# One more weight buffer for the experts: a gate rebuilt late, and SwiGLU's intermediate values left in PSUM

## The chip, the cores and the metric

The kernel runs on one core of a Trainium2 chip. The metric is device microseconds for one execution. Three runs of the kernel before took 1690.12, 1691.52 and 1692.07 us, median 1691.52.

## The reference, cut to what matters

Two transformer blocks over 256 tokens of width 1024, in fp32. The first has two attention branches and a mixture of 32 experts, four per token. The second is dense. The change touches the experts, and the gate `g_m` that multiplies their sum.

```
mod = silu(c) @ w_ada + b_ada
sh_a, sc_a, g_a, sh_m, sc_m, g_m = split(mod, 6)
x = x + g_a * merge(attention branches)
h = rmsnorm(x, norm_mlp) * (1 + sc_m) + sh_m
# for each of a token's 4 experts e
gate = min(h @ w_gate[e] + b_gate[e], 7)
up   = clip(h @ w_up[e] + b_up[e], -7, 7)
act  = (up + 1) * (gate * sigmoid(1.702 * gate))
y   += weight[e] * (act @ w_down[e] + b_down[e])
x = x + g_m * y                       # then the second block
```

## The kernel before, in words

**Stages.** The attention stage (to about 294 us of the profile) ends with the output projection and the router: `rwa` are the router's weights scaled by the gains, and L1233 holds its 16 matmuls, which read `rwa`. Then `moe()` runs the experts' stage (to about 1218 us), and `block2()` the second block.

**Experts.** They are done in 16 pairs. The two experts of a pair run side by side on the two column halves of TensorE (tiles `128*64`), 64 slots each. For pair p the program is written in this order: `gate(p)`, `scatter(p-2)`, `prep1`/`prep2(p+1)` (gather the next pair's tokens, matmuls L1341), `up(p)`, `prep3(p+1)` (two transposes L1358, two matmuls L1363), `down(p-1)`, `trans(p)` (transposes L1471). A scheduler reorders each engine's instructions by its own estimates; in most pairs it puts `prep3` between `gate(p)` and `up(p)`. Each of gate, up and down is 64 matmuls of 128x512 (L1431) into two PSUM banks, one for each half h of the 1024 columns.

**PSUM.** There are 8 banks. Four hold the running sum `acc` through the whole stage. The other four (`bank_a`) go round among gate, prep2, up, prep3, down and trans. A matmul that starts in a bank waits until the last reader of what stood there is done. The banks of `gate(p)` are next used by `prep3`: L1358 takes that of h=0, L1363 that of h=1. The banks of `up(p)` are next used by `down(p-1)`.

**SwiGLU.** After gate, for each h: a clip by VectorE (L1448, bank to SBUF tile `gs`), a sigmoid by ScalarE (L1449, `gs` to SBUF tile `e2`, shown as e), a product by VectorE (L1450). After up: a clip (L1459, bank to `e2`) and a fused (u+1)*g (L1460, `e2` and `gs` to `gs`). The last reader of a bank is thus the clip, L1448 or L1459.

**Weights.** Each gate, up or down of a pair is 8 loads of 1 MB, issued by SyncE's queue (SP) in one fixed list: gate(p), up(p), down(p-1). `fill()` issues the next load as soon as fewer than `room` tiles live. The first 12 expert loads go to the ring of 12 buffers, the next EXTRA (7) to the pool `more`, which `moe()` opens at L1262 in the space that the closed pools of the attention stage (`p1` among them) have left. I number the expert loads #1, #2, ...: #1 to #8 are gate(0), #9 to #16 up(0), #17 to #24 gate(1); #13 to #19 are the first in `more`. A load waits for the last user of its buffer's bytes, and all loads behind it on SP wait too. With 19 tiles, #20 waits until gate(0) frees a ring buffer.

**Overflow.** After pair 6 a branch (L1523) asks whether some expert has more than 64 tokens. At it SP waits until all its outstanding loads have landed before it issues the next.

**Gate g_m.** `gm_b` is g_m on all partitions. Its row is made in the attention stage: `add_row` adds `b_ada` (two small DMAs on ScalarE's queue, `brow`), `bcast_rows` splits it (mh, ml) and spreads it by four K=1 matmuls (L726, L727). It stays in the pool `keep` until L1659, after the last scatter. The same numbers stand as columns in `mod`.

**End of the stage.** `down(14)`, bias products L1409, scatter(14) L1514/L1515, `down_last` for pair 15 (L1498), in halves.

Of the kernel before, what the change touches and what calls it, by code (L numbers as in the profile page):

```python
# [25 lines left out]
AHEAD = 5  # L26
EXTRA = 7
OVER_AT = 6
# [47 lines left out]
def build(tc, I, out):  # L76
# [14 lines left out]
    def bank(which="a", dt=F32, shape=(128, 512)):  # L91
        return psp.tile(list(shape), dt, name="bank_" + which, tag="bank")
# [337 lines left out]
    mod = keep.tile([128, 3, 4, 4, 2], F32, name="mod")  # L430
    gm_b = keep.tile([128, D], F32, name="gm_b")
    kc = keep.tile([128, 256], F32, name="kc")
# [83 lines left out]
    def body():  # L516
# [142 lines left out]
        def ada_one():  # L659
# [36 lines left out]
            if g == 1:  # L696
                grow = cg.rearrange("p k t d -> p (k t d)")
                add_row(grow, 0, mrow, 0)
                late["row"] = grow
            if g == 2:  # L700
                add_row(mrow, 2, mrow, 1)
                late["rows"] = mrow

# [429 lines left out]
        while ada_queue:  # L1133
            ada_one()
        spreads = bcast_rows(ga_b, 0, late["row"]), bcast_rows(gm_b, 2, late["rows"])
        yb_hi, yb_lo = late["yb"][:, 0], late["yb"][:, 1]
# [121 lines left out]
    def moe(pl, parts, routed):  # L1258
# [44 lines left out]
        def token_weights():  # L1303
            V.tensor_reduce(out=sm[:, :, 0], in_=pr, axis=AX.X, op=OP.add)
            V.reciprocal(sm[:, :, 1], sm[:, :, 0])
            V.tensor_tensor(pr, pr, sm[:, :, 1:2].to_broadcast([128, 2, 4]), op=OP.mult)
            V.tensor_tensor(eq, eq, pr.unsqueeze(3).to_broadcast([128, 2, 4, 32]), op=OP.mult)
            V.tensor_reduce(out=wt, in_=eq.rearrange("p t k e -> p t e k"), axis=AX.X, op=OP.add)
            t = m1.tile([128, 2, 32], F32, name="w3t")
            V.tensor_copy(w3[:, :, 0], wt)  # L1310
            V.tensor_tensor(t, wt, w3[:, :, 0], op=OP.subtract)
            V.tensor_copy(w3[:, :, 1], t)
            V.tensor_tensor(t, t, w3[:, :, 1], op=OP.subtract)
            V.tensor_copy(w3[:, :, 2], t)
# [127 lines left out]
        def gate(p):  # L1442
            ps = expert_mm("gate", p, xg_of(p), "b_gate")
            g = scr([128, 1024], "gs", "wh")
            for h in range(2):
                g_ = g[:, 512 * h:512 * h + 512]
                s_ = m1.tile([128, 512], F32, name="e2", tag="e2")
                V.tensor_scalar(out=g_, in0=ps[h], scalar1=7.0, scalar2=None, op0=OP.min)  # L1448
                S.activation(s_, g_, AF.Sigmoid, scale=1.702)  # L1449
                V.tensor_tensor(g_, g_, s_, op=OP.mult)  # L1450
            state["g", p] = g

        def up(p):
            ps = expert_mm("up", p, xg_of(p), "b_up")
            g = state["g", p]
            for h in range(2):
                g_ = g[:, 512 * h:512 * h + 512]
                u_ = m1.tile([128, 512], F32, name="e2", tag="e2")
                V.tensor_scalar(out=u_, in0=ps[h], scalar1=7.0, scalar2=-7.0, op0=OP.min, op1=OP.max)  # L1459
                V.scalar_tensor_tensor(out=g_, in0=u_, scalar=1.0, in1=g_, op0=OP.add, op1=OP.mult)  # L1460

# [59 lines left out]
        def overflow():  # L1521
            nv = nc.values_load(nov[0:1, 0:1], min_val=0, max_val=16)
            with tc.If(nv > 0):  # L1523
                with tc.For_i(0, nv, 1):
                    oh = m1.tile([128, 96], F32, name="oh")
                    eb = m1.tile([128, 8], F32, name="eb")
                    V.scalar_tensor_tensor(out=oh, in0=oidx, scalar=it, in1=ov, op0=OP.is_equal, op1=OP.mult)
                    jk = m1.tile([128, 96], F32, name="jk")
                    V.scalar_tensor_tensor(out=jk, in0=oh, scalar=1.0, in1=eid, op0=OP.mult, op1=OP.mult,
# [6 lines left out]
                    ev = nc.sync.value_load(ei[0:1, 0:1], min_val=0, max_val=NE - 1)  # L1536
                    one = m1.tile([128, 32], F32, name="one")
                    V.tensor_scalar(out=one, in0=iota[:, :32], scalar1=eb[:, 0:1], scalar2=None, op0=OP.is_equal)
                    jk2 = m1.tile([128, 32], F32, name="jk2")
                    for tt in range(2):  # L1540
# [38 lines left out]
                    def block_bias(nm, h):  # L1579
                        t = scr([64, 512], "bb", "wl")  # L1580
                        nc.sync.dma_start(out=t, in_=sl[nm][bass.ds(ev, 1), 512 * h:512 * h + 512].to_broadcast([64, 512]))
                        return t

                    for h in range(2):
                        ps = block_mm("gate", lambda j: xo[:, j], h)
                        bt = block_bias("b_gate", h)
                        g_ = m1.tile([64, 512], F32, name="e2", tag="e2")
                        V.tensor_tensor(g_, ps, bt, op=OP.add)
                        V.tensor_scalar(out=g_, in0=g_, scalar1=7.0, scalar2=None, op0=OP.min)
                        s_ = scr([64, 512], "s_", "wl")  # L1590
                        S.activation(s_, g_, AF.Sigmoid, scale=1.702)
                        V.tensor_tensor(g_, g_, s_, op=OP.mult)
                        ps = block_mm("up", lambda j: xo[:, j], h)
                        bt = block_bias("b_up", h)
                        u_ = scr([64, 512], "u_", "wl")
                        V.tensor_tensor(u_, ps, bt, op=OP.add)
# [14 lines left out]
        for p in range(NPAIR):  # L1611
# [35 lines left out]
        for h in range(2):  # L1647
# [8 lines left out]
            for tt in range(2):  # L1656
                s = slice(512 * h, 512 * h + 512)
                t = m1.tile([128, 512], F32, name="e2", tag="e2")
                V.tensor_tensor(t, acc[tt][h], gm_b[:, s], op=OP.mult)  # L1659
                V.tensor_tensor(x_sb[:, tt, s], x_sb[:, tt, s], t, op=OP.add)  # L1660
# [418 lines left out]
```

## Time and profile before

| | |
|---|---|
| median of three runs | 1691.52 us |
| the profiled execution's own time | 1692.38 us |
| its span | 1690.7 us |
| PE busy | 1627.3 us (96%) |
| DVE, ACT busy | 694.0 us (41%), 465.5 us (28%) |
| HBM read | 534.75 MB, 317 GB/s over the span |
| 1 MB loads of w_up, w_down: median us from issue to landing | 19.5, 19.5 |

The page's 40 slices are 42.3 us each. The matmuls' ends are modelled, so PE's busy share doesn't say that PE is the bound; the starts are measured. A row of the timeline joins like instructions that follow each other: start, length, line, operation, tiles, count, and in brackets the idle time before the first with what ended it.

### The profile page before, as it was taken

What the parts mean: (1) busy time and instruction counts of PE and PEld (TensorE: products, weight loads), DVE (VectorE), ACT (ScalarE), POOL (GpSimd) and SP (SyncE); (2) the same over time, 40 slices, a digit from 0 to 9 for tenths busy, and PEclk for the clock granted to TensorE, in tenths of its full rate; (3) what the DMA queues carried; (4) which work ended last, traced back from release to release, by engine and by line L of the source; (5) the groups of instructions that cost most, each with busy time, mean ns of one, the idle gap of its engine ahead of it and who ended that gap; (6) DMA issues with size and microseconds to landing.
All of it is one profiled execution on the core that took longest, in us unless ns stands there. A gap on an engine that the chain in (4) does not pass through costs nothing. (4 is left out here: it accounts for less than half of the span.)

```text
span 1690.7 us, 22289 instructions
## 1 busy us (share of the span) xinstructions
PE 1627.3 (96%) x9091; PEld 1019.3 (60%) x9091; DVE 694.0 (41%) x1350; ACT 465.5 (28%) x769; POOL 88.9 (5%) x120
## 2 busy tenths in 40 slices
PE   8999999999999999899999999999999999999997
PEld 5877887444433443444344334434488899989996
DVE  4999986221111112111121121111367556665555
ACT  3445663010100100010001000000256445454443
POOL 3012200000000000000000000000004101100001
PEclk9999999999999999999999999999999999999999
DMA  9654668999999999999999999999963333565530
GB/s 377 252 189 150 208 249 358 391 424 425 425 426 424 426 425 425 383 425 424 426 425 425 425 425 426 425 423 425 403 244 112 133 132 124 184 218 181 176 146 25
DMA packets 117155, 537.29 MB, mean 318 GB/s; under 512 B 11882, under 2 KB 13622, under 8 KB 66874
## 3 DMA queue, kind: packets, MB, share of 16 engines
q1 hardware_dynamic: 112160, 532.19, 78.5%
q10 hardware_dynamic: 4458, 3.46, 0.7%
q8 instruction: 72, 1.18, 0.3%
q14 instruction: 33, 0.27, 0.0%
q0 software_dynamic: 432, 0.19, 0.0%
HBM read 534.75 MB, written 1.05 MB: 317 GB/s over the span
## 5 line engine op out<-in xcount | busy, mean ns | idle before, releaser
L1431 PE MATMUL bank_a<-w,xg 128*64 128x512 f32 x2048 | 520.4, 597 | 1.0 <-DMA w<-in_w_up_dram 1.0
L1431 PEld LDWEIGHTS bank_a<-w,xg 128*64 128x64 f32 x2048 | 183.5, 137 | 276.4 <-issue 254.6
L319 DVE TENSOR_TENSOR wl<-w,wh 128x1024 fp32r<-128x1024 f32 (+1 forms) x193 | 236.5, 1231 | 153.7 <-ACT wh L316 143.4
L316 ACT ACTIVATE wh<-w 128x1024 fp32r<-128x1024 f32 (+1 forms) x193 | 201.9, 1049 | 216.3 <-PE bank_a L389 88.1
L1431 PE MATMUL bank_a<-w,at 128*64 128x512 f32 x960 | 229.7, 595 | 8.0 <-DVE e L1459 5.3
L390 PE MATMUL bank_a<-hi,wl 128*128 128x256 f32 x640 | 180.3, 283 | 1.0 <-DVE wl L319 1.0
L388 PE MATMUL bank_a<-hi,wh 128*128 128x256 f32 x616 | 176.3, 287 | 1.1 <-ACT hi L474 0.6
L389 PE MATMUL bank_a<-lo,wh 128*128 128x256 f32 x616 | 174.3, 283 | 0.2 <-DVE lo L475 0.2
L1431 PEld LDWEIGHTS bank_a<-w,at 128*64 128x64 f32 x960 | 83.3, 137 | 149.6 <-issue 103.7
L513 ACT ACTIVATE y<-bank_a,ws 128x512 fp32r<-128x512 f32 x32 | 22.0, 688 | 444.8 <-PE bank_a L1431 430.1
L390 PEld LDWEIGHTS bank_a<-hi,wl 128*128 128x128 f32 x640 | 122.3, 192 | 1.4 <-DVE wl L319 1.4
L388 PEld LDWEIGHTS bank_a<-hi,wh 128*128 128x128 f32 x616 | 117.8, 192 | 3.2 <-issue 0.9
L389 PEld LDWEIGHTS bank_a<-lo,wh 128*128 128x128 f32 x616 | 118.1, 192 | 0.9 <-DVE lo L475 0.6
L514 DVE SCALAR_TENSOR_TENSOR y<-bank_a,ws,y 128x512 fp32r<-128x512 f32 x32 | 24.0, 751 | 221.9 <-ACT y L513 220.3
L1459 DVE TENSOR_SCALAR e<-bank_a 128x512 f32<-128x512 f32 x32 | 22.1, 691 | 185.7 <-PE bank_a L1431 184.1
L1449 ACT ACTIVATE e<-gs 128x512 f32<-128x512 f32 x32 | 20.2, 630 | 236.5 <-DVE gs L1448 224.9
L1341 PEld LDWEIGHTS bank_a<-gr,x_sb 128*128 128x128 f32 x512 | 64.2, 196 | 23.0 <-issue 19.5
L1448 DVE TENSOR_SCALAR gs<-bank_a 128x512 f32<-128x512 f32 x32 | 22.0, 691 | 134.5 <-PE bank_a L1431 114.2
L1341 PE MATMUL bank_a<-gr,x_sb 128*128 128x128 f32 x512 | 69.3, 286 | 0.7 <-DVE gr L1324 0.7
L1346 DVE TENSOR_SCALAR xg<-bank_a,abp 128x128 f32<-128x128 f32 x64 | 21.9, 404 | 106.9 <-PE bank_a L1341 106.9
L1349 ACT ACTIVATE xg<-bank_a,abp 128x128 f32<-128x128 f32 x64 | 24.3, 456 | 121.9 <-PE bank_a L1341 121.8
L354 PE MATMUL bank_b<-wh,hh 128*128 128x512 f32 x128 | 49.9, 390 | 0.0
(468 smaller groups left out, 2220.7 us busy)
## 6 DMA issues: line engine op xcount, KB each, us to landing
w<-in_w_up_dram SPq DMA_DIRECT2D x144, 1024.0 KB, 19.5
w<-in_w_down_dram SPq DMA_DIRECT2D x136, 1024.0 KB, 19.5
w<-in_w_gate_dram SPq DMA_DIRECT2D x128, 1024.0 KB, 17.9
w<-in_w_in_dram SPq DMA_DIRECT2D x44, 1024.0 KB, 8.0
w<-in_w_ada_dram SPq DMA_DIRECT2D x16, 1024.0 KB, 6.6
w<-in_w_ada_dram SPq DMA_DIRECT2D x16, 512.0 KB, 9.2
w<-in_w_out_dram SPq DMA_DIRECT2D x8, 1024.0 KB, 8.9
w<-in_w_down_dram SPq DMA_DIRECT2D x16, 512.0 KB, 10.9
```

Source lines behind the costliest of these rows:

```text
L316: split_last[0] = S.activation(r32(wh[:, :n]), t[:, o:o + n], AF.Copy)
L319: V.tensor_tensor(r32(wl[:, :n]), t[:, o:o + n], wh[:, :n], op=OP.subtract)
L354: PE.matmul(o, r32(sh), r32(mh), start=first, stop=False)
L388: PE.matmul(o, r32(wh[:, k, c]), r32(hi[:, j]), start=j == 0 and m % 2 == 0, stop=False)
L389: PE.matmul(o, r32(wh[:, k, c]), r32(lo[:, j]), start=False, stop=False)
L390: PE.matmul(o, r32(wl[:, k, c]), r32(hi[:, j]), start=False, stop=j == 7 and m % 2 == 1)
L513: S.activation(r32(hi), src, AF.Copy, scale=scale)
L514: V.scalar_tensor_tensor(out=r32(lo), in0=src, scalar=scale, in1=hi, op0=OP.mult, op1=OP.subtract)
L1341: PE.matmul(ps[:, k], x_sb[:, tt, o:o + 255:2], d["gr"][:, tt].rearrange("p e s -> p (e s)"), start=tt == 0, stop=tt == 1)
L1349: S.activation(xg[:, j], ps[:, k], AF.Identity, bias=abp_[:, 1, j:j + 1], scale=abp_[:, 0, j:j + 1])
L1431: state["mm"] = PE.matmul(ps[h][64 * ab:64 * ab + 64], lhs(j, ab), w[ab][:, e, 512 * h:512 * h + 512], start=bias is None and j == 0, stop ...
L1459: V.tensor_scalar(out=u_, in0=ps[h], scalar1=7.0, scalar2=-7.0, op0=OP.min, op1=OP.max)
```

## The change

EXTRA goes from 7 to 8, so that 20 tiles live. To free the space: `gm_b` moves from `keep` to `p1` (only as the accumulator of its column sums; in `p1` it stands between `ga_b` and `rwa`), and `gate_rows()` makes it anew at p=15 from `mod`: per half one VectorE copy that repeats the columns, four 128x128 matmuls with the identity, one ScalarE copy to `gm_b`. `add_row` for g_m and its `bcast_rows` go. The tile `e2` goes: the sigmoid is written to the bank that the clip has read, and the clip of up stays in its bank. `w3t` and the scratch of the overflow loop move into other tiles.

```diff
-EXTRA = 7
+EXTRA = 8
-    gm_b = keep.tile([128, D], F32, name="gm_b")
         ga_b = p1.tile([128, D], F32, name="ga_b")
+        gm_b = p1.tile([128, D], F32, name="gm_b")
         rwa = p1.tile([128, 8, 32], F32, name="rwa")
-            if g == 2:
-                add_row(mrow, 2, mrow, 1)
-                late["rows"] = mrow
-        spreads = bcast_rows(ga_b, 0, late["row"]), bcast_rows(gm_b, 2, late["rows"])
+        spreads = (bcast_rows(ga_b, 0, late["row"]),)
@@ gate(p)
-                s_ = m1.tile([128, 512], F32, name="e2", tag="e2")
                 V.tensor_scalar(out=g_, in0=ps[h], scalar1=7.0, scalar2=None, op0=OP.min)
-                S.activation(s_, g_, AF.Sigmoid, scale=1.702)
-                V.tensor_tensor(g_, g_, s_, op=OP.mult)
+                S.activation(ps[h], g_, AF.Sigmoid, scale=1.702)
+                V.tensor_tensor(g_, g_, ps[h], op=OP.mult)
@@ up(p)
-                V.tensor_scalar(out=u_, in0=ps[h], scalar1=7.0, scalar2=-7.0, op0=OP.min, op1=OP.max)
-                V.scalar_tensor_tensor(out=g_, in0=u_, scalar=1.0, in1=g_, op0=OP.add, op1=OP.mult)
+                V.tensor_scalar(out=ps[h], in0=ps[h], scalar1=7.0, scalar2=-7.0, op0=OP.min, op1=OP.max)
+                V.scalar_tensor_tensor(out=g_, in0=ps[h], scalar=1.0, in1=g_, op0=OP.add, op1=OP.mult)
+        def gate_rows():
+            gm_b = late["gm"] = m2.tile([128, D], F32, name="gm_b", tag="xg")
+            rest = late["rest"] = m2.tile([128, 2, 512], F32, name="rest", tag="xg")
+            for h in range(2):
+                rd = rest[:, h].rearrange("p (i n) -> p i n", i=4)
+                V.tensor_copy(rd, mod[:, 2, :, 2 + h, 0].unsqueeze(2).to_broadcast([128, 4, 128]))
+                ps = bank("a")
+                for i in range(4):
+                    PE.matmul(ps[:, 128 * i:128 * i + 128], rd[:, i], ident, start=True, stop=True)
+                S.copy(gm_b[:, 512 * h:512 * h + 512], ps)
...
                     bias_products()
+                    gate_rows()
```

Three places show how it moves instructions. The first is SP's queue at loads #13 to #20. In a row stand the line, the operation, the tile with its source, and the counters waited for (DVE, PE, Pool, Activation: engines; DMAHW, DMASW: earlier DMAs). Before:

```order
L206 DMA w_3173<-in_w_up_dram 128x2048 [waits DMASW3_49,DMASW4_49,DMASW2_49,DMAHW1_49,DMASW1_49,PE_49]
L206 DMA w_3175<-in_w_up_dram 128x2048 [waits DMAHW2_49,Pool_49]
L206 DMA w_3177<-in_w_up_dram 128x2048 [waits DMAHW3_49]
L206 DMA w_3179<-in_w_up_dram 128x2048 [waits DMAHW4_49]
L206 DMA w_3181<-in_w_gate_dram 128x2048 [waits DMAHW5_49,DVE_49,PE_49]
L206 DMA w_3183<-in_w_gate_dram 128x2048 [waits DVE_49,DMAHW6_49,PE_49,Activation_49]
L206 DMA w_3185<-in_w_gate_dram 128x2048 [waits DMAHW7_49]
L206 DMA w_3338<-in_w_gate_dram 128x2048 [waits DMAHW0_49,PE_49]
```

The same eight loads now:

```order
L206 DMA w_3156<-in_w_up_dram 128x2048 [waits DMAHW7_49,DVE_49,PE_49]
L206 DMA w_3158<-in_w_up_dram 128x2048 [waits DMAHW0_49,Pool_49]
L206 DMA w_3160<-in_w_up_dram 128x2048 [waits DMAHW1_49]
L206 DMA w_3162<-in_w_up_dram 128x2048 [waits DMAHW2_49]
L206 DMA w_3164<-in_w_gate_dram 128x2048 [waits DMAHW3_49,DVE_49]
L206 DMA w_3166<-in_w_gate_dram 128x2048 [waits DMAHW4_49,DVE_49,Activation_49]
L206 DMA w_3168<-in_w_gate_dram 128x2048 [waits DMAHW5_49]
L206 DMA w_3170<-in_w_gate_dram 128x2048 [waits DMASW4_49,DMASW3_49,DMAHW6_49,DMASW2_49,DMASW1_49]
```

The waits for the software DMAs have gone from #13 to #20, and #13 now waits for VectorE. In the built program the pool `more` begins lower: #13's buffer is bytes 163616 to 171808 of each partition, over `ga_b` (161024 to 165120), `gm_b` and `rwa` (169216 to 170240); before it was 171040 to 179232, over `rw` and the small tables behind `rwa`. #13's counts are those of L1242, which reads `ga_b`, and of the last router matmul (L1231, which was L1233). Before, #13's PE count was that of the small matmuls L1206, and the last router matmul stood at #18. #20 no longer waits for PE.

The second place is TensorE between gate and up of pair 2. Before:

```order
L1431 MATMUL bank_a_3754<-w_3651,xg_3586 64x512
L1358 LDWEIGHTS gb_3829
L1358 MATMUL bank_a_3918<-kh_80,gb_3829 128x128 [waits DVE_49]
L1358 LDWEIGHTS gb_3829
L1358 MATMUL bank_a_3918<-kh_80,gb_3829 128x128
L1363 LDWEIGHTS gb_3829
L1363 MATMUL bank_a_3923<-w3_3307,gb_3829 128x96 [waits DVE_49]
L1363 LDWEIGHTS gb_3829
L1363 MATMUL bank_a_3923<-w3_3307,gb_3829 128x96
L1431 MATMUL bank_a_3858<-w_3653,xg_3586 64x512 [waits DMAHW5_49]
```

The same place now (L1356 and L1361 were L1358 and L1363, L1429 was L1431):

```order
L1429 MATMUL bank_a_3730<-w_3619,xg_3564 64x512
L1429 MATMUL bank_a_3832<-w_3629,xg_3564 64x512 [waits DMAHW3_49]
L1429 MATMUL bank_a_3833<-w_3629,xg_3564 64x512
L1356 LDWEIGHTS gb_3803 [waits DVE_49]
L1356 MATMUL bank_a_3890<-kh_79,gb_3803 128x128 [waits PE_49]
L1356 LDWEIGHTS gb_3803
L1356 MATMUL bank_a_3890<-kh_79,gb_3803 128x128
L1361 LDWEIGHTS gb_3803 [waits DVE_49]
L1361 MATMUL bank_a_3895<-w3_3292,gb_3803 128x96 [waits PE_49]
L1361 LDWEIGHTS gb_3803
L1361 MATMUL bank_a_3895<-w3_3292,gb_3803 128x96
L1429 MATMUL bank_a_3832<-w_3631,xg_3564 64x512 [waits DMAHW4_49]
```

Two instructions of up, both for the same expert of the pair (tile w_3629), have moved ahead of prep3. Each wait for VectorE is for the last reader of gate's bank, the clip before and the product now.

The third place is TensorE at the end of the stage, before and now:

```order
L1431 MATMUL bank_a<-w,xg 64x512 x32
L1431 MATMUL bank_a<-w,at 64x512 x2
L1471 MATMUL bank_a<-ident,gs 128x128 x8
L1431 MATMUL bank_a<-w,at 64x512 x30
L1409 MATMUL bank_b<-bd,wtt 128x512 x4
L1514 MATMUL bank_b<-y,sc 128x512
L1515 MATMUL bank_b<-y,sc 128x512
```

```order
L1429 MATMUL bank_a<-w,xg 64x512 x30
L1429 MATMUL bank_a<-w,at 64x512 x32
L1407 MATMUL bank_b<-bd,wtt 128x512 x4
L1486 MATMUL bank_a<-ident,rest 128x128 x8
L1467 MATMUL bank_a<-ident,gs 128x128 x8
L1523 MATMUL bank_b<-y,sc 128x512
L1524 MATMUL bank_b<-y,sc 128x512
```

The eight transposes of pair 15 have moved from within down(14) to behind it, and the eight matmuls of `gate_rows` stand before them.

## Rows read from the trace of the kernel before

**Rows 1.** What the DMA engines moved, GB/s in 40 slices of the span.
```profile
GB/s 377 252 189 150 208 249 358 391 424 425 425 426 424 426 425 425 383 425 424 426 425 425 425 425 426 425 423 425 403 244 112 133 132 124 184 218 181 176 146 25
```

**Rows 2.** Timeline of PE, pair 2 and the start of pair 3 (columns as told above).
```profile
407.05 0.24 PE L1363 MATMUL bank_a<-w,gb 128*128 128x96 bf16 x2 [0.56 <-DVE gs L1448]
407.23 14.01 PE L1431 MATMUL bank_a<-w,xg 128*64 128x512 f32 x64
...
422.68 13.95 PE L1431 MATMUL bank_a<-w,at 128*64 128x512 f32 x62 [0.45 <-DVE e L1459]
...
465.29 0.24 PE L1363 MATMUL bank_a<-w,gb 128*128 128x96 bf16 x2 [0.56 <-DVE gs L1448]
```

**Rows 3.** Timeline of DVE beside rows 2.
```profile
405.45 0.69 DVE L1448 TENSOR_SCALAR gs<-bank_a 128x512 f32<-128x512 f32 x1 [4.31 <-PE bank_a L1431]
406.31 0.69 DVE L1448 TENSOR_SCALAR gs<-bank_a 128x512 f32<-128x512 f32 x1 [0.17 <-PE bank_a L1431]
406.92 0.68 DVE L1450 TENSOR_TENSOR gs<-gs,e 128x512 f32<-128x512 f32 x1
...
420.41 0.69 DVE L1459 TENSOR_SCALAR e<-bank_a 128x512 f32<-128x512 f32 x1 [11.42 <-PE bank_a L1431]
421.13 0.69 DVE L1460 SCALAR_TENSOR_TENSOR gs<-e,gs 128x512 f32<-128x512 f32 x1
421.93 0.69 DVE L1459 TENSOR_SCALAR e<-bank_a 128x512 f32<-128x512 f32 x1
```

**Rows 4.** Timeline of ACT beside rows 2.
```profile
406.23 0.63 ACT L1449 ACTIVATE e<-gs 128x512 f32<-128x512 f32 x1 [13.56 <-DVE gs L1448]
```

**Rows 5.** Waits of PE, 300 to 1190 us: total us, times, longest us.
```profile
PE bank_a L1363 <- DVE gs L1448: 6.2, 11, 0.6
PE bank_a L1431 <- DVE e L1459: 5.3, 11, 0.8
```

**Rows 6.** Timeline of PE, pairs 10 and 14.
```profile
866.39 0.25 PE L1363 MATMUL bank_a<-w,gb 128*128 128x96 bf16 x2 [0.56 <-DVE gs L1448]
...
1101.49 0.24 PE L1363 MATMUL bank_a<-w,gb 128*128 128x96 bf16 x2 [0.56 <-DVE gs L1448]
```

**Rows 7.** Timeline of SP's queue around the start of the experts' stage.
```profile
272.64 2.52 SPq L206 DMA_DIRECT2D w<-in_w_up_dram  x5
...
285.35 0.81 SPq L206 DMA_DIRECT2D w<-in_w_gate_dram  x2
297.77 0.80 SPq L206 DMA_DIRECT2D w<-in_w_gate_dram  x2
```

**Rows 8.** Waits of SP's queue, 284 to 286 us.
```profile
SPq L206 <- PE bank_b L1233: 1.6, 1, 1.6
```

**Rows 9.** Windows: us, engines' busy us, granted clock, DMA share, GB/s.
```profile
296.00:298.00 2.00, 2.00 (x12) 0.56 (x9) 0.00 (x0) 0.00 (x0) 0.00 (x0) 1.00 0.00 0
```

**Rows 10.** Timeline of PE and DVE behind the overflow branch.
```profile
689.26 4.04 PE L1341 MATMUL bank_a<-gr,x_sb 128*128 128x128 f32 x32
697.62 0.41 PE L1422 MATMUL bank_a<-b_up,sel 96*64 96x512 bf16 x2 [4.32 <-DVE gs L1448]
698.22 0.61 PE L1422 MATMUL bank_a<-b_up,sel 96*64 96x512 bf16 x2 [0.19 <-DVE gs L1448]
...
696.88 1.29 DVE L1448 TENSOR_SCALAR gs<-bank_a 128x512 f32<-128x512 f32 x2 [20.31 <-SPq L1523]
```

**Rows 11.** Timeline of PE at the end of the experts' stage.
```profile
1153.86 9.05 PE L1431 MATMUL bank_a<-w,xg 128*64 128x512 f32 x36
...
1172.68 0.73 PE L1471 MATMUL bank_a<-ident,gs 128*128 128x128 f32 x4
...
1174.85 7.63 PE L1431 MATMUL bank_a<-w,at 128*64 128x512 f32 x32
...
1193.04 3.69 PE L1409 MATMUL bank_b<-bd,wtt 32*128 32x512 f32 x8
```

**Rows 12.** Timeline of PE at the K=1 matmuls of `bcast_rows`.
```profile
231.54 0.41 PE L727 MATMUL bank_b<-ml,ones 1*128 1x512 f32 x4
```

More of the change, by code (lines that the diff above doesn't have):

```diff
@@ L1308, in token_weights @@
             V.tensor_reduce(out=wt, in_=eq.rearrange("p t k e -> p t e k"), axis=AX.X, op=OP.add)
-            t = m1.tile([128, 2, 32], F32, name="w3t")
+            t = lg
             V.tensor_copy(w3[:, :, 0], wt)
@@ L1457, in up @@
                 g_ = g[:, 512 * h:512 * h + 512]
-                u_ = m1.tile([128, 512], F32, name="e2", tag="e2")
-                V.tensor_scalar(out=u_, in0=ps[h], scalar1=7.0, scalar2=-7.0, op0=OP.min, op1=OP.max)
-                V.scalar_tensor_tensor(out=g_, in0=u_, scalar=1.0, in1=g_, op0=OP.add, op1=OP.mult)
+                V.tensor_scalar(out=ps[h], in0=ps[h], scalar1=7.0, scalar2=-7.0, op0=OP.min, op1=OP.max)
+                V.scalar_tensor_tensor(out=g_, in0=ps[h], scalar=1.0, in1=g_, op0=OP.add, op1=OP.mult)
         mid_last = [None]
@@ L1478, in down_out @@
             state["y", p, h] = (yh, yl)
+        late = {}
+        def gate_rows():
[8 more added lines that the diff above has]
+                S.copy(gm_b[:, 512 * h:512 * h + 512], ps)
         def at_of(p):
@@ L1524, in overflow @@
                 with tc.For_i(0, nv, 1):
-                    oh = m1.tile([128, 96], F32, name="oh")
+                    few = scr([128, 256], "few", "wl")
+                    oh, jk, one, jk2 = few[:, 0:96], few[:, 96:192], few[:, 192:224], few[:, 224:256]
                     eb = m1.tile([128, 8], F32, name="eb")
                     V.scalar_tensor_tensor(out=oh, in0=oidx, scalar=it, in1=ov, op0=OP.is_equal, op1=OP.mult)
-                    jk = m1.tile([128, 96], F32, name="jk")
                     V.scalar_tensor_tensor(out=jk, in0=oh, scalar=1.0, in1=eid, op0=OP.mult, op1=OP.mult,
@@ L1536, in overflow @@
                     ev = nc.sync.value_load(ei[0:1, 0:1], min_val=0, max_val=NE - 1)
-                    one = m1.tile([128, 32], F32, name="one")
                     V.tensor_scalar(out=one, in0=iota[:, :32], scalar1=eb[:, 0:1], scalar2=None, op0=OP.is_equal)
-                    jk2 = m1.tile([128, 32], F32, name="jk2")
                     for tt in range(2):
@@ L1579, in block_bias @@
                     def block_bias(nm, h):
-                        t = scr([64, 512], "bb", "wl")
-                        nc.sync.dma_start(out=t, in_=sl[nm][bass.ds(ev, 1), 512 * h:512 * h + 512].to_broadcast([64, 512]))
-                        return t
+                        t = scr([64, 1024], "bb", "wl")
+                        nc.sync.dma_start(out=t[:, 0:512],
+                                          in_=sl[nm][bass.ds(ev, 1), 512 * h:512 * h + 512].to_broadcast([64, 512]))
+                        return t[:, 0:512], t[:, 512:1024]
                     for h in range(2):
[L1585 to L1588, printed above, removed]
+                        g_ = block_mm("gate", lambda j: xo[:, j], h)
+                        bt, s_ = block_bias("b_gate", h)
+                        V.tensor_tensor(g_, g_, bt, op=OP.add)
                         V.tensor_scalar(out=g_, in0=g_, scalar1=7.0, scalar2=None, op0=OP.min)
-                        s_ = scr([64, 512], "s_", "wl")
                         S.activation(s_, g_, AF.Sigmoid, scale=1.702)
@@ L1593, in overflow @@
                         ps = block_mm("up", lambda j: xo[:, j], h)
-                        bt = block_bias("b_up", h)
-                        u_ = scr([64, 512], "u_", "wl")
+                        bt, u_ = block_bias("b_up", h)
                         V.tensor_tensor(u_, ps, bt, op=OP.add)
@@ L1641, in moe @@
         limit[0] = len(quarters)
+        gm_b, rest = late["gm"], late["rest"]
         def features(h):
@@ L1657, in moe @@
                 s = slice(512 * h, 512 * h + 512)
-                t = m1.tile([128, 512], F32, name="e2", tag="e2")
+                t = rest[:, 0]
                 V.tensor_tensor(t, acc[tt][h], gm_b[:, s], op=OP.mult)
@@ L1664, in moe @@
             for tt in range(2):
-                part_sq(parts, tt, h, x_sb[:, tt, 512 * h:512 * h + 512], m1.tile([128, 512], F32, name="sq", tag="e2"))
+                part_sq(parts, tt, h, x_sb[:, tt, 512 * h:512 * h + 512], rest[:, 1])
         ph.close()
```

## The prediction

> **What bounds the kernel now.** I read the page's traffic row first. From about 300 to 1190 us it stands near 425 GB/s [rows 1], which looks like a stage bound by weights: a load of 1 MB (1.0486 million bytes) takes 2.47 us at that rate, 24 of them a pair's 59.2 us. But the starts of TensorE's instructions say something else for most of it. L1363 comes once a pair, and from pair 2 to pair 3 it is 465.29 - 407.05 = 58.24 us [rows 2], less than the loads need. Inside a pair the matmuls follow each other, 64 in 14.01 us. So TensorE is the bound there, and it eats into the lead that the loads won earlier; from pair 10 to 14 the mean is (1101.49 - 866.39) / 4 = 58.78 us [rows 6], so the lead is used up in these pairs, and the end waits for loads. Then I read what TensorE waits for within a pair: twice for VectorE, 0.56 us before L1363 and 0.45 us at the start of down [rows 2], eleven times each [rows 5]. Both are waits for a PSUM bank. Last, SP's queue at the start of the stage: loads #12 to #16 go out from 272.64, #18 and #19 at 285.35, #20 at 297.77 [rows 7], and the DMA engines stand still between 296 and 298 [rows 9].
>
> So three clocks run side by side: TensorE's order, the loads' line, and at the overflow branch SP's drain.
>
> **Banks held longer (the main term).** The clip was the last reader of gate's banks, now it is the product, behind a sigmoid. In pair 2 the second clip ends at 406.31 + 0.69 = 407.00, and L1363 starts at 407.05 [rows 2, 3]. Now the second sigmoid can follow the second clip, as the first does, 0.09 behind it and 0.63 long [rows 3, 4], to 407.72; the product follows as before, 0.06 behind it and 0.68 long, to 408.46; L1361 starts at 408.51 in place of 407.05: 1.46 us later. The two instructions of up that stand ahead of it now don't make up for that: both belong to one column half of the array, and the other half can't start its 32 matmuls before L1361 is through. Rows of before show this with down: two matmuls started early, and the 62 others still took 13.95 us from the second bank's release [rows 2].
>
> In down, the second bank was free at 421.93 + 0.69 = 422.62, and PE went on at 422.68. Now the order clip, fused product, clip, fused product ends one product later: a step is 0.72 (420.41 to 421.13), so the third starts at 421.86, the fourth at 422.58 and ends at 423.27, and PE goes on at 423.33: 0.65 later [rows 2, 3]. Together 2.1 us a pair, in the eleven pairs that show both waits (2 to 6 and 9 to 14, [rows 5]); 58.24 becomes 60.3, more than the loads' 59.2. No row shows ScalarE writing PSUM. Bounds: 0.55 to 0.75 for a sigmoid that takes 0.63 into SBUF, so, with as much again for the wait in down, 1.9 to 2.3 us a pair.
>
> The Trainium skill's page "ScalarE: Activation LUTs" (Step-by-step: what each stage is for) says that ScalarE writes PSUM with less latency than SBUF; by that alone the sum would be at the lower bound, 1.9 us a pair. The skill's page "PSUM — Partial Sum Buffer" (Summary: rules for kernel authors) says "Evacuate promptly", which speaks against the change as the 0.56 us waits do; I hold with those.
>
> **The extra buffer.** #13's new buffer lies over `rwa`, so #13 waits for the last router matmul. That is what #18 waits for now, and it goes out at 285.35 [rows 7, 8]. #13 went out at about 273.2. All behind it in the queue wait as well, #14 to #20. Both #13 now and #20 before go out on an idle line, and after #13 seven more loads follow at 2.47 each: #20 lands as if it went out at 285.35 + 7 x 2.47 = 302.6, against 297.77. So the loads' line is 4.9 us late, 4.4 with what the stage before gains (below). With #13 at its old time the twentieth buffer would make it one load, 2.47 us, early, out of the gap at 296.
>
> **Smaller terms.** Before the stage four K=1 matmuls go: one group of four spans 0.41 [rows 12], take -0.45 with the small waits about it. VectorE and ScalarE lose the adds and splits beside them, which I take at nothing, since other work of theirs lies there and TensorE is the busy one; bounds -1 to +1, an instruction of 0.69 like the clips [rows 3] gone from, or come into, a chain that TensorE waits for. `gate_rows` adds eight fp32 matmuls, 16 passes on PE: 32 of L1341's take 4.04 us [rows 10], so 2.0; its copies on VectorE and ScalarE have the bias products (3.69 us, [rows 11]) as cover. The transposes of pair 15, 2.17 us of PE between up and down (1172.68 to 1174.85, [rows 11]), now stand behind it and cost some 1.05, like 8 passes of L1341. The new order of the last scatter, -0.7 (0 to -1.5).
>
> **The sum.** TensorE's order: -0.45, then five pairs before the overflow, 5 x 2.1: +10.05 when it reaches it. There it had finished its gathers at 689.26 + 4.04 = 693.30 and waited 4.32 us, because VectorE's clip waited for SP's drain to 696.88 [rows 10]. Now the gathers end at 703.35. The drain holds one load more, since 20 tiles live, on a line 4.4 late: clip at 696.88 + 4.4 + 2.47 = 703.75. But up's bias matmuls now wait for the second product, 3.0 us after the first clip starts (405.45 to 408.46): they go at 706.8 against 698.22 [rows 10], 8.6 late. Take 8.0, since what PE loses behind its idle time may shrink. Then six more pairs, 12.6: 20.6. Against it, what TensorE has waited for loads since pair 10, and now needn't: 4 x 0.54 = 2.1 up to pair 14; in pair 15, up took 1172.68 - 1153.86 = 18.8 where 14.0 and 1.5 of waits would do: 3.3; down 1193.04 - 1174.85 = 18.2 for 13.95: 4.2; and some 2 in between that rows don't show well. 11.6, and 2.17 for the transposes that left: +6.8 when the bias products begin. On the loads' line alone that would be +4.4, so TensorE's order decides. Behind it +2.0, +1.05, -0.7. Sum +9.2 on the profiled execution's 1692.38: 1701.6. That execution lies 0.86 above the median, so 1700.7 against 1691.52.
>
> Range of this case: +-0.2 us a pair over eleven pairs, the overflow's 7 to 8.6, the tail and the small instructions before the stage: 1697 to 1705.
>
> **Rivals.**
> (a) The loads decide. If the longer bank waits are smaller than worked out, or fall into waits for weights, the loads' line sets the end: +4.4, +2.0, +1.05, -0.7: +6.8, 1698.3. For it: the line at 425 GB/s; against: the 58.24 us.
> (b) The buffer does what it says. #13 goes out near 273, the gap at 296 closes, the loads are 2.47 early, and the bank waits are hidden: -2.47 - 0.45 + 2.35 = -0.6, 1691. For it: the bubble. Against: #13's wait for the last router matmul. The Trainium skill's page "Perfetto Trace Analysis" (Optimization Strategy) says that gaps that come again and again can mean too little room for the next tile; by that this one, which a twentieth buffer is to fill, would speak for (b), but it stands once, at the start.
> (c) Faster. As (b), and `gate_rows` and the transposes lie in the time in which TensorE waits for the last loads of down(14) (4.2 us), which takes 3.05 from the tail: -3.6, 1687.9. It decides from the point where the bias products and `gate_rows` are issued ahead of the last loads. Against: they stand behind all of down(14) on PE's queue.
> (d) Every term at its upper end: 2.3 us a pair (six pairs behind the overflow, +1.2), the overflow at 8.6 (+0.6), +1 before the stage: 9.2 + 2.8 = 12.0, 1703.5. For it: a bank that two engines use in turn has no row here; against: nothing but the single durations.
>
> **How the numbers follow.** Forecast 0.60, (a) 0.19, (b) 0.08, (c) 0.04, (d) 0.09. A change of 0.2% (3.4 us) is what a measurement can tell from none. The forecast, (a) and (d) are slower by more than that, but for some of (a)'s and the forecast's lower tails, 0.03: slower 0.85; same 0.11; faster 0.04. The range leaves out (b), (c) and the ends of the others: 1696.5 to 1705.
>
> **What would show it.** In the profile after: L1361 waits about 2 us for VectorE in eleven pairs where L1363 waited 0.56; the period of a pair is near 60.3 where it was 58.24; TensorE's waits for weights at the end of the stage shrink or vanish; #13 goes out at about 285, the DMA engines have little to do between #12 and it, and the gap at 296 is gone; `gate_rows` and the transposes stand behind the bias products at some 3 us. I am wrong if the period stays at 58.2 to 59.2 (then (a) or (b)), if #13 goes out near 273 (then (b)), or if the bank waits do not grow.

## The result, and the profile after

The kernel after took 1703.37 us (median of 6 runs, 1701.66 to 1705.02), the one before 1691.78 beside it; the ratio is 1.0065, 95% interval 1.0055 to 1.0075. So it is slower by 11 us. The profiled execution took 1702.21 (span 1700.4) against 1692.38 (span 1690.7).

The traffic row of the page, against [rows 1]: the seventh slice (some 254 to 297 us) falls from 358 to 259, the eighth rises from 391 to 425, and the dip at the overflow stays.

```profile
GB/s 379 246 191 151 207 278 259 425 424 425 424 425 425 426 425 425 382 425 425 425 426 425 425 425 424 424 379 426 403 261 100 140 120 138 176 216 184 175 154 25
```

TensorE in pair 2 and at the start of pair 3, with VectorE and ScalarE beside it, against [rows 2 to 4] (lines have moved: L1363 is L1361 now, L1431 is L1429, L1448 to L1450 are L1445 to L1447, L1459 and L1460 are L1455 and L1456):

```profile
406.86 0.28 PE L1356 MATMUL bank_a<-kh,gb 128*128 128x128 bf16 x2 [1.12 <-DVE gs L1447]
407.62 0.26 PE L1361 MATMUL bank_a<-w,gb 128*128 128x96 bf16 x2 [0.48 <-DVE gs L1447]
...
422.47 1.04 PE L1429 MATMUL bank_a<-w,at 128*64 128x512 f32 x2 [0.71 <-PE bank_a L1429]
423.85 13.95 PE L1429 MATMUL bank_a<-w,at 128*64 128x512 f32 x62 [0.34 <-DVE gs L1456]
...
467.84 0.26 PE L1361 MATMUL bank_a<-w,gb 128*128 128x96 bf16 x2 [0.48 <-DVE gs L1447]
...
404.66 0.69 DVE L1445 TENSOR_SCALAR gs<-bank_a 128x512 f32<-128x512 f32 x1 [4.31 <-PE bank_a L1429]
405.52 0.69 DVE L1445 TENSOR_SCALAR gs<-bank_a 128x512 f32<-128x512 f32 x1 [0.17 <-PE bank_a L1429]
406.13 1.44 DVE L1447 TENSOR_TENSOR gs<-gs,bank_a 128x512 f32<-128x512 f32 x2
...
420.94 0.70 DVE L1455 TENSOR_SCALAR bank_a<-bank_a 128x512 f32<-128x512 f32 x1 [12.60 <-PE bank_a L1429]
421.67 0.69 DVE L1456 SCALAR_TENSOR_TENSOR gs<-bank_a,gs 128x512 f32<-128x512 f32 x1
...
406.24 0.60 ACT L1446 ACTIVATE bank_a<-gs 128x512 f32<-128x512 f32 x1 [0.20 <-DVE gs L1445]
```

L1361 starts 0.05 us behind the end of the second product (406.13 + 1.44 = 407.57), as it did behind the clip before. The pair period is 467.84 - 407.62 = 60.22 us where it was 58.24. What TensorE waits for, 300 to 1190 us, against [rows 5] (total us, times, longest us):

```profile
PE bank_a L1356 <- DVE gs L1447: 10.7, 11, 1.1
PE bank_a L1429 <- PE bank_a L1429: 7.8, 11, 0.7
PE bank_a L1361 <- DVE gs L1447: 5.2, 11, 0.5
PE bank_a L1420 <- DVE gs L1447: 4.4, 2, 4.2
PE bank_a L1429 <- DVE gs L1456: 3.7, 11, 0.3
```

The products L1447 and L1456 stand where the clips stood, and no wait for a weight load is left. SP's queue at the start of the stage (timeline), its two waits ahead of #13, and the window of 296 to 298, against [rows 7], [rows 8] and [rows 9] in this order:

```profile
272.11 14.60 SPq L206 DMA_DIRECT2D w<-in_w_up_dram  x5
```

```profile
SPq L206 <- DVE m L1242: 8.3, 1, 8.3
...
SPq L206 <- PE bank_b L1231: 4.0, 1, 4.0
```

```profile
296.00:298.00 2.00, 2.00 (x12) 0.70 (x10) 0.00 (x0) 0.00 (x0) 0.00 (x0) 1.00 0.98 406
```

#12 goes out at 272.11; #13, the second of the five, at 284.75. It waits 8.3 us for L1242, which reads `ga_b`, and then 4.0 for the router's last matmul. The gap at 296 is gone, but a longer one stands ahead of it. The timeline of PE and DVE at the overflow, and of PE at the end of the stage, against [rows 10] and [rows 11]:

```profile
698.25 4.04 PE L1339 MATMUL bank_a<-gr,x_sb 128*128 128x128 f32 x32
706.50 0.41 PE L1420 MATMUL bank_a<-b_up,sel 96*64 96x512 bf16 x2 [4.21 <-DVE gs L1447]
...
704.34 1.29 DVE L1445 TENSOR_SCALAR gs<-bank_a 128x512 f32<-128x512 f32 x2 [18.78 <-SPq L1532]
...
1201.19 3.69 PE L1407 MATMUL bank_b<-bd,wtt 32*128 32x512 f32 x8
1204.81 2.05 PE L1486 MATMUL bank_a<-ident,rest 128*128 128x128 f32 x16
1206.70 1.12 PE L1467 MATMUL bank_a<-ident,gs 128*128 128x128 f32 x8
...
1209.62 7.94 PE L1507 MATMUL bank_a<-w,at 128*64 128x512 f32 x34
```

Up's bias matmuls behind the overflow go 706.50 - 697.62 = 8.88 us later than before, the bias products 8.15 (1201.19 against 1193.04), the down products of pair 15 9.37 (1209.62 against 1200.25); the span ends 9.7 later.

### The profile page after: what moved, and what is told of

It is laid out like the page before. It is cut to its first block, busy times and chain, and to the rows that moved or that the text cites. A ratio compares the mean times of both kernels' runs of the same rounds, so it can differ in the third digit from the quotient of the medians.

```text
span 1700.4 us, 22309 instructions
## 1 busy us (share of the span) xinstructions
PE 1624.5 (96%) x9103; PEld 1017.9 (60%) x9103; DVE 691.6 (41%) x1349; ACT 463.3 (27%) x768; POOL 88.9 (5%) x120
## 3 DMA queue, kind: packets, MB, share of 16 engines
HBM read 534.75 MB, written 1.05 MB: 315 GB/s over the span
## 4 chain that ended last, share of the span: by engine, by line
PE 53%; DVE 3%; ACT 1%; issue 1%; POOL 0%; DVEq 0%; ACTq 0%
PE bank_a L1429 23%; PE bank_a L388 4%; PE bank_a L390 4%; PE bank_a L389 4%; PE bank_b L354 2%; PE bank_b L355 2%; PE bank_b L356 2%; PE bank_a L1339 2%; PE bank_a L1507 1%; PE bank_a L355 1%; PE bank_a L356 1%; PE bank_a L354 1%; PE bank_b L1523 1%; PE bank_a L1945 1%; DVE wl L319 1%; PE bank_a L1947 1%
## 5 line engine op out<-in xcount | busy, mean ns | idle before, releaser
L1429 PE MATMUL bank_a<-w,xg 128*64 128x512 f32 x2048 | 520.9, 597 | 0.0
L1429 PEld LDWEIGHTS bank_a<-w,xg 128*64 128x64 f32 x2048 | 177.3, 137 | 283.0 <-issue 266.9
L1429 PE MATMUL bank_a<-w,at 128*64 128x512 f32 x960 | 224.5, 594 | 12.7 <-PE bank_a L1429 7.8
L1429 PEld LDWEIGHTS bank_a<-w,at 128*64 128x64 f32 x960 | 88.9, 137 | 144.8 <-issue 124.3
L1455 DVE TENSOR_SCALAR bank_a<-bank_a 128x512 f32<-128x512 f32 x32 | 22.2, 695 | 201.0 <-PE bank_a L1429 201.0
L1446 ACT ACTIVATE bank_a<-gs 128x512 f32<-128x512 f32 x32 | 19.1, 601 | 206.1 <-DVE gs L1445 206.1
L1445 DVE TENSOR_SCALAR gs<-bank_a 128x512 f32<-128x512 f32 x32 | 22.0, 691 | 129.4 <-PE bank_a L1429 110.6
```

Of the source, the lines that this page charges most:

```text
L1429: state["mm"] = PE.matmul(ps[h][64 * ab:64 * ab + 64], lhs(j, ab), w[ab][:, e, 512 * h:512 * h + 512], start=bias is None and j == 0, stop ...
```

## The experiments

Ratios are to the kernel before, timed beside them; "late" is the position of load #13. Two theories at first: banks (theory 1), or load #13 and the tail (theory 2).

**1. The PSUM edit alone** (on the kernel before, 19 buffers):

```diff
-                s_ = m1.tile([128, 512], F32, name="e2", tag="e2")
-                S.activation(s_, g_, AF.Sigmoid, scale=1.702)
-                V.tensor_tensor(g_, g_, s_, op=OP.mult)
+                S.activation(ps[h], g_, AF.Sigmoid, scale=1.702)
+                V.tensor_tensor(g_, g_, ps[h], op=OP.mult)
 # and in up(): the clip writes ps[h], the fused product reads it
```

> The kernel before with one part of the change alone: sigmoid and clipped values stay in PSUM; 19 buffers, the gate's rows as before. Theory 1 (TensorE waits for banks whose last reader is now the product): the waits for L1447's kind of product return, the pair period goes from 58.24 to 60.2 us from pair 2 on, TensorE no longer waits for any weight load between 290 and 1205 us, and the time rises by +6 to +9 us, to 1698 to 1701. Theory 2 (load 13 of the stage that goes out 12 us late, and the gate's rows at the end, decide): neither part is in here, so the time stays within 1.5 us of 1691.8.

Measured: 1.0024 (1.0013 to 1.0036), about 4 us. TensorE's four waits for banks of gate and up (L1358, two in down, L1363) are those of after to 0.1 us (10.6, 7.8 and 3.7, 5.2 in all), and none is for a load. Theory 2 alone fails, for there is a cost without #13; but the cost is below theory 1's.

**2. SBUF again, first try** (on after): the sigmoid into the next pair's gathered rows, the clipped values of up into scratch.

```diff
+            nx = state["xg", p + 1] = m2.tile([128, 8, 2 * CAP], F32, name="xg", tag="xg")
+                s_ = nx[:, 4 * h:4 * h + 4].rearrange("p a b -> p (a b)")
+                S.activation(s_, g_, AF.Sigmoid, scale=1.702)
```

> The kernel after with 20 buffers, but the sigmoid goes to SBUF again (into the next pair's gathered rows, which are not yet written) and the clipped values of up into a free scratch buffer, so that the clip is again the last reader of each bank. Load 13 still goes out late, the gate's rows stay at the end. Theory 1: the pair period returns to about 58.2 us, waits for weight loads come back in the last pairs, and the loads' line, 4.4 us late, decides: 1695 to 1699 us. Theory 2: nothing that decides is touched, 1702 to 1704.5 us.

**3. Load #13 early, first try** (on after): one unused tile takes the lowest buffer.

```diff
+        extra[0].tile([128, 2048], F32, name="w", tag="w")
         set_room(SLOTS + EXTRA)
```

> The kernel after, with the buffer that lies over the router's weights given to the last of the eight extra loads instead of the first, so that load 13 goes out at about 273 us instead of 284.8. Banks are held as in after. Theory 1: TensorE is behind its banks and waits for no load, so an earlier line of loads brings 0 to 2 us: 1701.4 to 1703.4. Theory 2: 4.4 us or more come back: 1696 to 1699.

**4. Both.**

> The kernel after with both edits: sigmoid and clipped values in SBUF, load 13 early; 20 buffers and the gate's rows at the end remain. Theory 1: period 58.2 us, loads' line as in the kernel before or a little ahead of it, the gate's rows 2 us in the tail partly inside waits for loads: 1690 to 1694 us, 4 to 7 us below the run with SBUF alone. Theory 2: the same as the run with load 13 early alone, 1696 to 1699.

Measured: 1.0058 (1.0042 to 1.0075), 1.0061 (1.0047 to 1.0075), 1.0048 (1.0032 to 1.0063). None of the three did what it was made for. In 2 and 4 prep2 had to wait until the product had read the scratch, and the period was 59.1, not 58.2. In 3 and 4 load #13 still went out at 286.76 and 284.46, since the unused tile's wait was passed on to the next load: in 3 the queue still waits 8.3 us for L1242 and 4.0 for the router's last matmul ahead of #13. What they did show: behind the drain the first load goes out at 702.99 in 2 and 704.23 in 4, whose banks are no longer held by the product, at 704.61 in after, and at 695.86 in experiment 1, with held banks and #13 early (697.18 in the kernel before). So the drain follows the loads, not the banks. That gave theory 3: two lines, of which the later counts at the overflow and at the end, with the tail behind.

**5. 19 buffers in the kernel after** (`EXTRA = 7`).

> The kernel after with 19 buffers (EXTRA 7): banks held by the products and the gate's rows at the end stay, load 13 goes out early again. Theory 3, from the four runs so far: the end of the experts' stage is the later of two lines, the loads' (late by load 13 and by one more load ahead of the overflow's drain) and TensorE's (banks held, +2 us a pair, forgiven up to the overflow where TensorE waits anyway); the gate's rows add 2 to 2.5 us behind both. Here: clip after the drain within 0.5 us of before, bias products +5.5 as with the PSUM edit alone, end 2.4 us behind that run: 1698.5 to 1700.5. Theory 2 (load 13 and the tail): tail alone, 1694 to 1696. If the gate's rows cost nothing: as the PSUM edit alone, 1696.6.

Measured: 1.0055 (1.0040 to 1.0070). A miss: load #13 went out at 284.74, late with 19 buffers too. So it is not the number of buffers that delays it. The change takes `gm_b`, `e2` and some small tiles out of what lies under the extra buffers; the first of them begins lower, over the router's weights, whether there are seven or eight. It isn't `e2` alone, for experiment 1 takes that out as well and has #13 early; the other tiles were not tried apart. What the 20th buffer does cost when #13 is late stands at the drain, where the clip comes 2.88 us sooner with 19 buffers than in after (701.46 against 704.34):

```profile
701.46 1.29 DVE L1445 TENSOR_SCALAR gs<-bank_a 128x512 f32<-128x512 f32 x2 [16.04 <-SPq L1532]
```

**6. SBUF again, second try**: after, with the sigmoid and the clipped values in the two scratch buffers of the down products, once `scatter(p-2)` has read these.

```diff
-            gate(p)
+            gate(p)                       # matmuls only
             if p > 1 and p != OVER_AT + 1:
                 scatter(p - 2)
+            gate_out(p)                   # sg = scr([128, 1024], "sg", "wl"); clip, sigmoid into sg, product
```

> The kernel after with 20 buffers and load 13 late, sigmoid and clipped values in the two scratch buffers of the down products, which are free at that time, so that neither the banks nor the gathered rows are held (the first try held the gathered rows: period 59.1). Theory 1 (banks alone decide): period 58.2, 1691 to 1694. Theory 3: period 58.2 up to the overflow, drain +7 us as in after, then the loads' line +4.5 us at the bias products and 2.4 us of tail: 1698 to 1701. Theory 2: the same as theory 3.

Measured: 1.0041 (1.0026 to 1.0056). The median is 1700.25, so theory 1 alone (1691 to 1694) fails. The period is 58.05 us ahead of the overflow; the wait before L1361 is that of before (6.2 us in all), the one in down is shorter (2.8 for 5.3). Then TensorE stands 12.57 us for the drain. PE and DVE at the overflow, and PE at the end of the stage:

```profile
689.82 4.04 PE L1339 MATMUL bank_a<-gr,x_sb 128*128 128x128 f32 x32
706.43 1.24 PE L1420 MATMUL bank_a<-b_up,sel 96*64 96x512 bf16 x4 [12.57 <-DVE gs L1449]
...
705.68 1.29 DVE L1449 TENSOR_SCALAR gs<-bank_a 128x512 f32<-128x512 f32 x2 [30.25 <-SPq L1537]
...
1195.87 3.65 PE L1429 MATMUL bank_a<-w,at 128*64 128x512 f32 x12 [1.72 <-DMA w<-in_w_down_dram]
1199.44 3.70 PE L1407 MATMUL bank_b<-bd,wtt 32*128 32x512 f32 x8
```

It reaches the overflow 8.4 us ahead of after (689.82 against 698.25) and leaves it together with it (706.43 against 706.50). At the end TensorE waits 4.8 us for loads again (3.8 of down, 1.0 of up), and the bias products stand 6.40 later than before.

**7. Load #13 early, second try**: after, with the lowest buffer as a pool of its own that is filled last.

```diff
-        extra.append(pool("more", bufs=EXTRA, st=ph, reuse_waits="tile"))
+        low = pool("more1", st=ph, reuse_waits="tile")
+        extra.extend([pool("more", bufs=EXTRA - 1, st=ph, reuse_waits="tile"), low])
 # fill() takes the pool of seven first, the single one when seven are out
```

> The kernel after with banks held, the 20th buffer as a pool of its own under the other seven, so that only the last of the eight extra loads waits for the router's weights and load 13 goes out at about 273 us (the first try left the wait on load 13: out at 286.8 us). Theory 3: drain only +2.5 us (one more load ahead of it), banks decide: bias products +6, tail +2.4: 1700 to 1702. Theory 2: 4.4 us come back in full and the rest is tail: 1695 to 1698.

**8. Both second tries.**

> Both edits: 20 buffers, load 13 early, sigmoid and clipped values in the scratch buffers, gate's rows at the end. Theory 3: drain +2.5 us, bias products -0.5 to +1 (the loads' line is that of before), tail +2.4: 1693 to 1696. Theory 1 without a price for the 20th buffer: 1690 to 1692.5. A theory by which a 20th buffer costs time by itself at the drain: 1697 or more.

Measured: 1.0027 (1.0016 to 1.0037) with #13 early, 0.9999 (0.9988 to 1.0009) with both. SP's queue, PE and DVE of experiment 7, and its bias products:

```profile
271.80 2.55 SPq L206 DMA_DIRECT2D w<-in_w_up_dram  x5
...
697.90 4.04 PE L1343 MATMUL bank_a<-gr,x_sb 128*128 128x128 f32 x32
701.87 0.62 PE L1424 MATMUL bank_a<-b_up,sel 96*64 96x512 bf16 x4
...
697.52 1.29 DVE L1449 TENSOR_SCALAR gs<-bank_a 128x512 f32<-128x512 f32 x2 [12.31 <-SPq L1536]
...
1194.45 3.70 PE L1411 MATMUL bank_b<-bd,wtt 32*128 32x512 f32 x8
```

The five loads go out in 2.55 us, the clip stands at 697.52, 0.64 behind that of [rows 10], and TensorE, 8.6 us late by its banks (697.90 against 689.26), runs through the overflow without a wait: the idle time that was there swallows half of the lag (701.87 against 697.62). The clip of theory 3 was to be 2.5 late; with #13 early the 20th load costs the drain little. It goes out at 291.04, and the gap at 296 gets shorter, but doesn't close. The windows of 292 to 302, in the kernel before and in experiment 7:

```profile
292.00:302.00 10.00, 10.00 (x57) 4.48 (x58) 3.54 (x14) 2.10 (x4) 0.00 (x0) 1.00 0.52 199
292.00:302.00 10.00, 10.00 (x57) 4.45 (x57) 3.47 (x14) 0.81 (x2) 0.00 (x0) 1.00 0.72 273
```

Measured by the 425 GB/s around it, an estimate from these rows, the gap is 5.3 us before and 3.6 now. With this the four corners are there:

| | #13 early | #13 late |
|---|---|---|
| values in SBUF | 0.9999 | 1.0041 |
| values in PSUM | 1.0027 | 1.0065 (after) |

Late loads cost 0.0042 and 0.0038 (7.1 and 6.4 us), banks 0.0028 and 0.0024 (4.7 and 4.1 us), each difference uncertain by 2.4 to 3.1 us (after is from its own comparison with before). Within that they add up.

**9. Bias products ahead of down(14)**, in the kernel before; **10. bias products and gate's rows there**, on top of experiment 8:

```diff
             if p == NPAIR - 1:
                 with tc.issue_after(state["mm"].ins):
                     bias_products()
+                    gate_rows()           # in experiment 10
+            if p > 0:
+                down(p - 1)
-            (the same lines, behind down(p - 1))
```

> The kernel before with one move: the four bias products stand ahead of the down products of pair 14 instead of behind them (they need only the token weights and the down bias). In the kernel before TensorE waits there for loads (1.93 and 0.62 us in down, 0.80 for the up product's result, and the scatter behind runs at half the granted clock, 3.58 us). Theory 3 (the loads' line decides the end of the stage): 2 to 3.5 us of the 3.63 us of bias products vanish in these waits: 1.0 to 3.5 us faster than before. If TensorE's own work decided the end: no change within 0.5 us.

> The run with both edits (20 buffers, load 13 early, values in scratch buffers), and bias products and the gate's rows moved ahead of the down products of pair 14. That run waits there 0.41 + 0.57 + 0.55 + 2.04 us for loads of down, and 3.70 + 2.05 us of bias products and gate's rows come behind. Theory 3: 3 to 4 us of them vanish in the waits: 1688.5 to 1691, faster than both kernels. If the waits only move to a later load: 1692 to 1694.

Measured: 0.9978 (0.9970 to 0.9987) and 0.9971 (0.9958 to 0.9984), in medians 1690.02 and 1686.95 against 1693.45. The timeline of PE at the end of the stage in experiment 10, and what is left there of its waits for loads (290 to 1205 us):

```profile
1170.65 3.69 PE L1411 MATMUL bank_b<-bd,wtt 32*128 32x512 f32 x8
1174.28 2.05 PE L1495 MATMUL bank_a<-ident,rest 128*128 128x128 f32 x16
1176.26 5.36 PE L1433 MATMUL bank_a<-w,at 128*64 128x512 f32 x20
...
1195.91 7.94 PE L1516 MATMUL bank_a<-w,at 128*64 128x512 f32 x34
```

```profile
PE bank_a L1433 <- DMA w<-in_w_up_dram: 1.0, 2, 0.5
PE bank_a L1433 <- DMA w<-in_w_down_dram: 0.5, 1, 0.5
```

In experiment 8 the waits for down were these (300 to 1190 us):

```profile
PE bank_a L1433 <- DMA w<-in_w_down_dram: 4.1, 5, 2.0
```

3.6 of the 4.1 us are filled, and the last down products start at 1195.91 against 1201.84 in experiment 8. Experiment 9, the move alone, brings nearly as much: the 0.0007 between it and experiment 10 are uncertain by 0.0016.

**11 and 12. Experiment 10 once more, and with 19 buffers** (`EXTRA = 7`, #13 early).

> The fastest kernel so far once more (20 buffers, load 13 early, values in scratch buffers, bias products and gate's rows ahead of the down products of pair 14), to stand beside the run with 19 buffers on the same chip: 1686 to 1690.

> The same with 19 buffers. Theory 3 (a 20th buffer is worth the gap of about 2.4 us that it fills in the loads' line at 296 us, as far as the loads still decide; TensorE then waits 0.5 + 1.0 us for loads at the end): 1 to 3 us slower than with 20, 1688 to 1692. If the 20th buffer is worth nothing: the same within 0.7 us. If it costs (one more load ahead of the drain): 1 to 2 us faster.

Measured: 0.9962 (0.9948 to 0.9977) with 20, 0.9982 (0.9972 to 0.9992) with 19. With 20 it is faster by 0.0020, 3.4 us, uncertain by 3. That is not the 20th buffer alone, for with 19 the load #16 went out late as well (at 281.29; in experiment 10 all five are out by 275.53). The version with 20 buffers (1686.08 and 1686.95) beats both kernels; that it beats experiment 9 isn't shown.

## Why the prediction came out as it did

The time was inside the range, 2.7 us above the forecast. The profiled execution, which the sum was made for, was forecast at 1701.6 and took 1702.21, 9.8 us more than that of before where 9.2 were worked out. That it is so close is partly luck. The bias products came 8.15 later for +6.8, the tail came out at 2.4 for 2.35, and behind the stage 0.8 us were given back that the sum doesn't have; the medians of six runs lie 11.6 apart.

- **Banks held longer: right.** 60.3 us a pair forecast, 60.22 measured. From the start of gate's first clip to L1361 it is 2.96 us (404.66 to 407.62) where it was 1.60, 1.36 more for the 1.46 worked out. From up's first clip to the 62 matmuls of down it is 2.91 (420.94 to 423.85) where it was 2.27, 0.64 more for 0.65. The sigmoid took 0.60 us into PSUM where [rows 4] have 0.63 into SBUF. Most of the wait stands a matmul earlier than the prediction put it, at L1356 (1.12 us), and in down in two parts (0.71 and 0.34). The profile puts the 0.71 down to TensorE itself; they end 0.11 behind the first fused product (421.67 + 0.69), which is the last reader of that bank. The Trainium skill's page "ScalarE: Activation LUTs" (Step-by-step: what each stage is for) says that ScalarE reaches PSUM with less latency than SBUF; the 0.60 against 0.63 agrees. The Trainium skill's page "PSUM — Partial Sum Buffer" (Summary: rules for kernel authors) says "Evacuate promptly"; the 4.1 to 4.7 us of the corners agree.
- **Load #13: right in place, in size and in what it waits for.** 285.35 forecast, 284.75 measured; clip behind the drain 703.75 forecast, 704.34 measured. The two parts of its lateness, 4.4 for the line and 2.47 for one load more, were 4.58 (701.46 in experiment 5 against 696.88) and 2.88. But the prediction puts all this under the extra buffer, and it isn't the 20th buffer that moves #13 (experiment 5), it is the room that `gm_b` and the small tiles left.
- **The overflow: right in its mechanism, a little short.** Gathers to end at 703.35, they ended at 702.29; up's bias matmuls at 706.8, they went at 706.50. The prediction worked out 8.6 late and took 8.0, since what TensorE loses behind its idle time might shrink. It was 8.88 and didn't shrink: the next L1361 stands 8.88 later too (722.99 against 714.11).
- **"On the loads' line alone that would be +4.4, so TensorE's order decides": right in its order, short on both sides.** In after TensorE waits for no load at the end of the stage, and the bias products come 8.15 later for +6.8. Experiment 6 has the loads' line alone: +6.40 for +4.4. So TensorE's order adds 1.75 there for the 2.4 forecast; by the ratios banks cost 4.1 with #13 late, uncertain by 3.
- **What that comparison hides: most of the loss is the loads'.** They set when the overflow lets TensorE go (706.43 with banks free against 706.50), as the prediction's own 706.8 has it, and TensorE's order carries that to the end. Ahead of the overflow the banks cost nothing with #13 late, since the drain waits longer anyway. Behind it they add 2 us a pair, but experiment 6 waits for its last loads where after doesn't: at L1361 of pair 14 the two lie 12.59 apart (1108.04 against 1120.63), at the bias products 1.75. By the forecast's numbers an early #13 would have brought 3.45 us (TensorE free at 703.35 instead of 706.8). Experiment 7 brought 4.63 there (701.87), 6.74 at the bias products (1194.45 against 1201.19) and 6.4 of the 11 by the ratios, uncertain by 2.4; the 2 us between are the lower clock behind the idle time (last section), which the forecast has no number for.
- **Rival (a)** was the case of banks without a price, +6.8; experiment 6 is that case and measured +6.9 (0.0041 of 1693). **Rival (b)** was the case of an early #13 with banks hidden, -0.6; experiment 8 is that case, though the gap at 296 didn't close: -0.2.
- **Rival (c)** was -3.6, of which -3.05 for `gate_rows` and the transposes in the waits for the last loads. Experiment 10, with the bias products moved as well, measured -4.9 and -6.4 (0.9971 and 0.9962), and against experiment 8 0.0028, 4.7 us, uncertain by 2.8.
- **Rival (d)** gives 1703.5, next to the median of 1703.37, but not by its terms. Only the overflow came out above its end (8.88 for 8.6). A pair took 1.98 more, not 2.3, and before the stage it wasn't +1: the router's matmuls start 0.55 sooner (282.83 against 283.38), gate(0) 0.23 later (294.37 against 294.14). So the forecast's -0.45 didn't reach the stage either.
- **Tail: right in sum, by luck in its parts.** `gate_rows` 2.05 (forecast 2.0), transposes 1.12 (1.05). From the bias products to the last down products it grew by 8.43 - 7.21 = 1.2, not 2.35: the scatter took 2.0 us at a granted clock of 1.00 where the kernel before took 3.6 at 0.50. That is a clock that happened to be up, for in experiment 7, with after's order there, it fell to 0.50 in `gate_rows` (last section). The last down products took 1.2 us longer to their end, in five pieces between other matmuls where it had been three.

## What to carry to other kernels

Who keeps a value in PSUM to free SBUF pays with the time to the last reader: count it in the places where TensorE already waits for a bank. Who frees SBUF moves what is allocated behind it: look which earlier tile the first buffer of the next stage now lies on, since one waiting load on an in-order queue holds up all behind it. And where two lines meet at several places, give each its own run before calling one the bound; where the end waits for loads, put independent work ahead of those waits.

## What the runs showed of the hardware

At the drain, work of TensorE behind its idle time ran at the lower of its two clock levels. In experiment 6, behind the 12.57 us (windows: us, busy us of PE, PEld, DVE, ACT and POOL, granted clock, DMA share, GB/s):

```profile
705.90:708.00 2.10, 1.57 (x6) 0.65 (x7) 1.95 (x4) 1.54 (x4) 0.00 (x0) 0.50 0.47 101
708.00:710.00 2.00, 2.00 (x7) 0.60 (x5) 2.00 (x7) 1.03 (x3) 0.00 (x0) 0.50 0.97 406
...
712.00:714.00 2.00, 2.00 (x10) 0.66 (x8) 0.00 (x0) 0.00 (x0) 0.00 (x0) 0.88 0.99 418
```

0.50 is 1.2 GHz. About 6 us of work were done at it, which costs some 3 us (an estimate: in experiment 6's timeline the next two matmuls of 128x512, side by side, go every 0.85 us there and every 0.43 at full clock). The window of 708 to 710 in after, behind 4.21 us of idle time, and in experiment 7, which has none there:

```profile
708.00:710.00 2.00, 2.00 (x8) 0.61 (x6) 1.21 (x6) 0.00 (x0) 0.00 (x0) 0.50 1.00 414
708.00:710.00 2.00, 2.00 (x12) 0.61 (x10) 0.00 (x0) 0.00 (x0) 0.00 (x0) 1.00 1.01 426
```

So the wait that went there gave back more than its own length: up's bias matmuls come 4.63 us sooner in experiment 7, and the next L1361 (L1365 there) 6.71 (716.28 against 722.99).

At the end of the stage no such rule comes out of the runs. In the kernel before the scatter behind the waits for down stood at 0.50 (1197 to 1200 us); in after, with no such wait ahead, the same matmuls ran at 1.00. But in experiment 7, with no such wait either, `gate_rows` stood at 0.50 (1199 to 1201 us) and took 3.30 us for 2.05. And in experiment 6 the scatter ran at 1.00 behind a wait of 1.72. What lowers the clock there stays open.
